# The last projection of a hybrid trunk: seven products over four pairs of output blocks in place of eight, with the outputs kept on chip

## The chip, the cores and the metric

The kernel runs on one core of one Trainium2 chip. A core has five engines that this text calls PE (TensorE, matrix products; its weight loads are shown apart as PEld), DVE (VectorE), ACT (ScalarE), POOL (GpSimd) and SP (SyncE, which here only issues transfers). Each engine works through its own list of instructions in order and waits at semaphores for the others. The metric is the time of one execution in microseconds (us); less is better.

## The reference, cut to what matters

One even layer, one odd layer and a final norm over 1024 positions of width 1024, all in float32. The change concerns the end: the odd layer's output projection with a 2048 x 1024 weight, the residual, and the final norm.

```python
def rmsnorm(x, g):
    xf = x.astype(jnp.float32)
    return xf * lax.rsqrt(jnp.mean(xf * xf, axis=-1, keepdims=True) + RMS_EPS) * g
...
    y = b_gate * conv * jax.nn.silu(g)
    return y @ w_out
...
            h_res = h_res + short_conv_mixer(h, sc_w_in[i], sc_conv_w[i], sc_conv_b[i], sc_w_out[i])
    return rmsnorm(h_res, final_g).astype(out_dtype)
```

## The kernel before

Everything is held transposed: channels on the 128 partitions, positions along the row. Every float32 operand of a product is split into a high part (one ACT copy that rounds) and a low part (one DVE subtraction), and each product of two 128-row blocks is three matmuls: high x high, high x low, low x high. `split_to` does a split (lines 81 and 82, or 84 and 85 with a factor). `tt` on line 229 is every plain two-input operation of DVE and POOL, so the tiles' names tell them apart.

The earlier stages already use seven products in place of eight for a 2 x 2 block product (`run_pairs`, the matmuls of line 686). They leave the odd layer's gated result y as sixteen blocks of 128 x 1024 in DRAM (`y2d`, stored by line 885). The last pair of blocks, 14 and 15, is finished by two DVE multiplications (tiles `K` and `t`) when the last projection has begun.

The last projection is a plain product. The positions are two halves of 512. For each half, and for each of eight output blocks m, two units run, one for each half of the 2048 input rows: a unit loads a weight block of 128 x 1024 from `scout` (line 97, issued by ACT), splits it (`wsplit`: `whi`, `wlo`), and runs 8 x 3 matmuls of 512 columns (`mm_j`, line 933) into one PSUM tile `acc`. `evac_j` then adds the residual block on DVE, squares it on ACT, applies the gain on ACT, and adds the squares up on DVE. The last block of the second half runs in two quarters of 256 columns (`mm_j7`, line 976), so that the norm of one quarter lies beside the products of the other. `rms_work` makes the norm: ones-vector matmuls (line 150), a short chain on DVE and ACT, a broadcasting matmul (line 168) and an ACT copy (line 169). `j_norm` scales and SP stores the result.

The order of everything is the order in which the code is written (`manual_schedule`): each engine's list is filled as the program text runs. In `steps`, while PE runs unit s, the others are given the split of unit s + 1, the load of unit s + 2, and the evacuation of unit s - 1.

Of the kernel before, what the change touches and what calls it, by code (L numbers as in the profile page):

```python
# [8 lines left out]
F32 = mybir.dt.float32  # L9
# [5 lines left out]
P = 128  # L15
T = 1024
# [11 lines left out]
def trunk(ctx: ExitStack, tc: tile.TileContext, a: dict, out: bass.AP):  # L28
# [44 lines left out]
    def act_tiles(k, shape=(T,)):  # L73
        t = act_slot(k, [P, 2, *shape])
        act[k] = (t[:, 0], t[:, 1])
        return act[k]

    def split_to(h, l, src, scale=None, e=None):

        if scale is None:  # L80
            A.activation(h, src, AF.Copy)  # L81
            (e or V).tensor_tensor(out=l, in0=src, in1=h, op=ALU.subtract)  # L82
        else:
            A.activation(h, src, AF.Copy, scale=scale)  # L84
            V.scalar_tensor_tensor(out=l, in0=src, scalar=scale, in1=h, op0=ALU.mult, op1=ALU.subtract)  # L85
# [142 lines left out]
    def tt(e, o, x, y, op):  # L228
        e.tensor_tensor(out=o, in0=x, in1=y, op=op)  # L229
# [689 lines left out]
    def mm_j(m, kk, half):
        def f(u, work):  # L920
            if kk == 0:
                J_["acc"] = acc_tile()
            acc = u.acc = J_["acc"]
            places = spread(work, 3)
            for k in range(8):
                if k in (2, 4, 6):
                    for g in next(places):
                        g()
                n = kk * 8 + k
                h, l = act[n // 2]  # L930
                w1, w2 = u.hi[:, k * P : k * P + P], u.lo[:, k * P : k * P + P]
                for i, (w, x) in enumerate(((w1, h), (w1, l), (w2, h))):
                    PE.matmul(acc[:, 0:512], lhsT=w, rhs=x[:, n % 2], start=n == 0 and i == 0, stop=n == 15 and i == 2)  # L933
        return f

    def fetch_j(m, half):
        def f():
            t = J_["h", m] = slot(f"t{m % 2}", [P, 512])
            LD.dma_start(t, hrd[m][:, 512 * half : 512 * half + 512])
        return f  # L940

    def evac_j(m, half):
        def f(u):
            if m == 0 and half == 0:
                J_["td"] = slot("td0", [P, 4, 512])
            if m % 2 == 0:
                if half and m == 6:
                    J_["o", half, 3] = J_["td"][:, 0:2]
                else:
                    J_["o", half, m // 2] = slot(f"t{2 + 4 * half + m // 2}", [P, 2, 512])  # L950
            o = J_["o", half, m // 2][:, m % 2]
            tt(V, o, u.acc[:, 0:512], J_["h", m], ALU.add)
            q = J_["td"][:, 3 if m == 0 else 2]
            A.activation(q, o, AF.Square)
            A.activation(o, o, AF.Copy, scale=gf[:, m : m + 1])
            if 0 < m:
                tt(V, J_["td"][:, 3], J_["td"][:, 3], q, ALU.add)
        return f
# [5 lines left out]
    def mm_j7(q):
        def f(u, work):
            acc = J_["acc7", q] = acc_tile()[:, 0:256]
            places = spread(work, 15)
            for n in range(16):
                if n:
                    for g in next(places):  # L970
                        g()
                w = units[idx["j", 1, 7, n // 8]]
                k, (h, l) = n % 8, act[n // 2]
                w1, w2 = w.hi[:, k * P : k * P + P], w.lo[:, k * P : k * P + P]
                for i, (wt, x) in enumerate(((w1, h), (w1, l), (w2, h))):
                    PE.matmul(acc, lhsT=wt, rhs=x[:, n % 2, quarter(q)], start=n == 0 and i == 0, stop=n == 15 and i == 2)  # L976
        return f

    def evac_j7(q):
        c = quarter(q)  # L980
        o = J_["o", 1, 3][:, 1, c]
        tt(V, o, J_["acc7", q], J_["h", 7][:, c], ALU.add)
        A.activation(J_["td"][:, 2, c], o, AF.Square)

    def j_rms(c, last):
        def sums():
            if c.start == 0:
                J_["rs"] = slot("rs", [P, 512])
            return [J_["td"][:, 3, c]] + ([J_["td"][:, 2, c]] if last else [])
        return rms_work(sums, lambda: J_["rs"][:, c], c.stop - c.start)  # L990

    def j_norm(half, i, c, e):

        n = c.stop - c.start
        o, r = J_["o", half, i], J_["rs"][:, c]
        if half and i == 3:
            V.scalar_tensor_tensor(out=o[:, 1, c], in0=o[:, 1, c], scalar=gf[:, 7:8], in1=r, op0=ALU.mult, op1=ALU.mult)
            tt(e, o[:, 0, c], o[:, 0, c], r, ALU.mult)
# [39 lines left out]
    for half in range(2):  # L1038
        for m in range(8):
            last = half and m == 7  # L1040
            add(("j", half, m, 0), Unit(scout[m], mm_j7(0) if last else mm_j(m, 0, half), fetch=fetch_j(7, 1) if last else None))
            add(("j", half, m, 1), Unit(scout[8 + m], mm_j7(1) if last else mm_j(m, 1, half),
                                        None if last else evac_j(m, half), fetch=None if last else fetch_j(m, half)))
# [186 lines left out]
    for k in range(4):  # L1230
# [9 lines left out]
    jA, jB, N_ = idx["j", 0, 0, 0], idx["j", 1, 0, 0], len(units)  # L1240
    sc_tail = {1: [lambda: first_of(jA)],
               2: [lambda: [y2_load(0, n, n + 2) for n in range(0, 14, 2)]],
               4: [lambda: [y2_split(0, n) for n in range(4)]],
               5: [lambda: wsplit(units[jA]), lambda: [y2_split(0, n) for n in range(4, 8)]]}
    for i in range(8):
        at(pre, jA + 3 + i, lambda i=i: y2_load(1, 2 * i, 2 * i + 2))
    at(post, jB - 2, lambda: [y2_split(1, n) for n in range(8)])
# [141 lines left out]
    for n in range(8, 12):
        y2_split(0, n)  # L1390

    def first_j():
        late = end2()
        for n in range(12, 14):
            y2_split(0, n)
        for n in range(14, 16):
            late[n - 14]()
            y2_split(0, n, H_["b"][n - 14][:, H0])

    steps(jA, N, first_j)  # L1400
    evac_j7(1)
    for f in rB[1]:
# [71 lines left out]
```

## Time and profile before

| | us |
|---|---|
| median of 3 runs (lowest, highest) | 1636.63 (1634.88, 1636.76) |
| the profiled execution: time | 1635.34 |
| the profiled execution: span from first to last instruction | 1633.5 |
| PE busy in the span | 1581.8 (97%) |
| DVE, ACT, POOL busy in the span | 1074.0, 550.4, 661.3 |
| the last projection and final norm, from its first matmul | 1438.2 to 1633.5 |

The profile is of one execution. Its span leaves out 1.8 us of the time around it. A busy PE is a PE with a matmul in flight; matmuls overlap, so the spacing of their starts tells the pace. A wait is shown in square brackets behind an instruction: how long its engine sat idle before it, and which instruction ended that.

### The profile page before, as it was taken

To read this page: it belongs to the slowest core of one execution; us is meant where nothing else is said; L and a number is where in the kernel's file an instruction comes from. 1 tells how busy PE (TensorE), PEld (TensorE's weight loads), DVE (VectorE), ACT (ScalarE), POOL (GpSimd) and SP (SyncE) were. 2 spreads that over 40 slices of the span, in tenths; PEclk is the share of its full clock that TensorE was granted. 3 is DMA by queue.
4 is the path that set the end of the run, shared out by engine and by line. 5 is a ranking of instruction groups with operands and counts; after the bars stand their busy time and mean duration, and the time that the engine had idled before them with its cause. 6 is when DMAs were issued, how large, how long until landed. Compare 5 with 4: busy or idle time off the path is not lost.

```text
span 1633.5 us, 19047 instructions
## 1 busy us (share of the span) xinstructions
PE 1581.8 (97%) x7186; PEld 1308.3 (80%) x7186; DVE 1074.0 (66%) x1249; ACT 550.4 (34%) x818; POOL 661.3 (40%) x636
## 2 busy tenths in 40 slices
PE   9899999998999999999879999999999999999997
PEld 7688888877888788888658888888888888878886
DVE  6545655688555776661798686968686777763543
ACT  5245211123443433341443232332333332343531
POOL 6852599707422533102455353534343535400001
PEclk9999999999999999999979999999999999999998
DMA  6242632214687432133201212112121212266353
GB/s 213 97 123 91 152 118 84 78 47 148 190 292 228 159 116 78 55 131 132 109 26 52 102 54 78 63 67 77 54 101 52 78 52 78 72 200 205 116 154 117
DMA packets 95035, 181.30 MB, mean 111 GB/s; under 512 B 16352, under 2 KB 52960, under 8 KB 94432
## 3 DMA queue, kind: packets, MB, share of 16 engines
q10 hardware_dynamic: 49664, 116.41, 22.1%
q1 hardware_dynamic: 45280, 63.68, 11.6%
q8 instruction: 57, 0.93, 0.2%
q14 instruction: 34, 0.28, 0.0%
HBM read 141.33 MB, written 42.93 MB: 113 GB/s over the span
## 4 chain that ended last, share of the span: by engine, by line
PE 59%; DVE 5%; issue 1%; DMA 1%; ACT 0%; ACTq 0%; DVEq 0%
PE acc L686 44%; PE acc L933 9%; PE acc L114 4%; PE acc L837 1%; DVE t L229 1%; DVE a L85 1%; DVE ws L82 1%; PE acc L976 1%; DVE a L82 0%; DMA t<-in_glu 0%; DMA hpd<-t 0%; PE aux L168 0%; DVE big L82 0%; ACTq L911 0%; PE aux L150 0%
## 5 line engine op out<-in xcount | busy, mean ns | idle before, releaser
L686 PE MATMUL acc<-a,ws 128*128 128x512 f32 x1920 | 451.3, 391 | 4.0 <-DVE LR L229 1.7
L686 PEld LDWEIGHTS acc<-a,ws 128*128 128x128 f32 x1920 | 361.8, 189 | 81.5 <-ACT a L81 3.1
L114 PE MATMUL acc<-a,whi 128*128 128x512 f32 x1440 | 393.3, 395 | 3.3 <-DVE t L229 2.6
L114 PEld LDWEIGHTS acc<-a,whi 128*128 128x128 f32 x1440 | 268.3, 189 | 58.9 <-issue 4.0
L229 POOL TENSOR_TENSOR t<-t,t 128x512 f32<-128x512 f32 (+2 forms) x81 | 145.6, 1797 | 294.5 <-DVE ws L82 183.7
L686 PE MATMUL acc<-big,ws 128*128 128x512 f32 x960 | 230.9, 396 | 11.6 <-DVE ws L82 4.7
L81 ACT ACTIVATE ws<-t 128x512 fp32r<-128x512 f32 x200 | 125.8, 630 | 338.7 <-PE acc L686 201.5
L82 DVE TENSOR_TENSOR wlo<-raw,whi 128x1024 fp32r<-128x1024 f32 (+2 forms) x89 | 117.2, 1320 | 181.7 <-ACT whi L81 181.7
L686 PEld LDWEIGHTS acc<-big,ws 128*128 128x128 f32 x960 | 182.7, 191 | 53.4 <-DVE ws L82 6.4
L114 PE MATMUL acc<-a,wlo 128*128 128x512 f32 x720 | 222.6, 390 | 0.0
L82 DVE TENSOR_TENSOR ws<-t,ws 128x512 fp32r<-128x512 f32 x200 | 181.5, 908 | 34.0 <-ACT ws L81 32.1
L114 PEld LDWEIGHTS acc<-a,wlo 128*128 128x128 f32 x720 | 136.0, 189 | 28.8
L81 ACT ACTIVATE whi<-raw 128x1024 fp32r<-128x1024 f32 (+2 forms) x89 | 86.7, 977 | 190.1 <-PE acc L114 120.9
L933 PE MATMUL acc<-a,whi 128*128 128x512 f32 x480 | 149.0, 391 | 1.5 <-ACT a L84 1.1
L229 DVE TENSOR_TENSOR t<-t,acc 128x512 f32<-128x512 f32 x134 | 91.1, 681 | 51.0 <-PE acc L686 51.0
L686 PE MATMUL acc<-td,ws 128*128 128x512 f32 x480 | 118.1, 395 | 0.3 <-DVE td L82 0.3
L686 PEld LDWEIGHTS acc<-td,ws 128*128 128x128 f32 x480 | 91.2, 190 | 21.2 <-issue 1.3
L933 PEld LDWEIGHTS acc<-a,whi 128*128 128x128 f32 x480 | 90.0, 188 | 21.6 <-ACT a L84 1.5
L229 POOL TENSOR_TENSOR t<-C,LR 128x1024 f32<-128x1024 f32 (+1 forms) x18 | 42.6, 2372 | 141.3 <-PE aux L491 62.3
L933 PE MATMUL acc<-a,wlo 128*128 128x512 f32 x240 | 93.8, 391 | 0.3 <-DVE wlo L82 0.3
L229 POOL TENSOR_TENSOR t<-t,rs 128x512 f32<-128x512 f32 x5 | 8.7, 1747 | 197.2 <-ACT rs L169 197.2
L229 POOL TENSOR_TENSOR raw<-raw,raw 128x512 f32<-128x512 f32 x20 | 26.7, 1337 | 121.1 <-DVE ws L82 121.0
(260 smaller groups left out, 1945.6 us busy)
## 6 DMA issues: line engine op xcount, KB each, us to landing
raw<-in_scin ACTq DMA_DIRECT2D x32, 512.0 KB, 4.4
t<-in_scin ACTq DMA_DIRECT2D x32, 512.0 KB, 4.2
raw<-in_scout ACTq DMA_DIRECT2D x32, 512.0 KB, 3.7
raw<-in_win ACTq DMA_DIRECT2D x29, 512.0 KB, 3.6
t<-ud ACTq DMA_DIRECT2D x16, 512.0 KB, 4.2
raw<-in_wout ACTq DMA_DIRECT2D x16, 512.0 KB, 3.9
big<-y2d ACTq DMA_DIRECT2D x15, 512.0 KB, 5.8
ud<-t SPq DMA_DIRECT2D x8, 512.0 KB, 3.1
```

The source lines that it names most:

```text
L81: A.activation(h, src, AF.Copy)
L82: (e or V).tensor_tensor(out=l, in0=src, in1=h, op=ALU.subtract)
L85: V.scalar_tensor_tensor(out=l, in0=src, scalar=scale, in1=h, op0=ALU.mult, op1=ALU.subtract)
L114: PE.matmul(acc[:, n * 512 : n * 512 + 512], lhsT=w, rhs=x[:, n * 512 : n * 512 + 512], start=first and i == 0, stop=last and i == 2)
L229: e.tensor_tensor(out=o, in0=x, in1=y, op=op)
L686: PE.matmul(bank, lhsT=wt, rhs=x[:, k], start=k == 0 and j == 0, stop=k == 3 and j == 2)
L837: PE.matmul(u.acc[:, hs], lhsT=w, rhs=x[:, hs], start=k == 0 and j == 0, stop=k == NK - 1 and j == 2)
L933: PE.matmul(acc[:, 0:512], lhsT=w, rhs=x[:, n % 2], start=n == 0 and i == 0, stop=n == 15 and i == 2)
L976: PE.matmul(acc, lhsT=wt, rhs=x[:, n % 2, quarter(q)], start=n == 0 and i == 0, stop=n == 15 and i == 2)
```

## The change

The projection is cut into 2 x 2 blocks. For a pair p of output blocks (2p and 2p + 1) the weight gives A11 (`scout[2p]`), A12 (`scout[8 + 2p]`), A21 (`scout[2p + 1]`) and A22 (`scout[9 + 2p]`); y gives B11 (blocks 0 to 7, first half of the positions), B12 (the same, second half), B21 (blocks 8 to 15, first half) and B22. Seven products of sums of these replace the eight plain ones. The sums of B serve all four pairs, so the order is product by product: product 1 for the four pairs, then 5, 7, 6, 4, 2 and 3 (`JT`). That makes 28 units of 8 x 3 matmuls; product 3 runs in two quarters of 256 columns, its four units twice, which makes 32 steps t = 0 to 31 (`j_slot`).

- `jb_sum`: the sums of B, in place, 8 operations of 128 x 512 for each of products 5, 7, 6 and 4. Half of them stand on POOL, half on DVE; those of product 4 are all on POOL. `jb_split` splits the result, two blocks in a step.
- `jw_sum`: the sums of A, one operation of 128 x 1024 for each of the 16 units of products 5, 7, 6 and 3, all on POOL. Units of products 1, 4 and 2 have none.
- `j_post`: adds a finished product from PSUM to the outputs it belongs to, which stay on chip (`JO`): one ACT copy for product 1; 1, 2, 3, 1, 1 and 1 DVE additions for products 5, 7, 6, 4, 2 and 3.
- `res_add`: the residual, one POOL addition of 128 x 1024 for each output block. `j_sq2`, `j_sq`, `j_norm`: squares, gain and norm as before, in other pieces.
- All loads of the stage are issued by SP instead of ACT, and the output is stored in 24 transfers in place of 12.

```diff
+    JT = (1, 5, 7, 6, 4, 2, 3)
...
+    def jb_sum(i, n, e):
+        if i == 5:
+            tt(e, x0(n), x1(n), x0(n), ALU.subtract)
+        elif i == 7:
+            tt(e, x1(n), b22(n), x1(n), ALU.subtract)
+        elif i == 6:
+            tt(e, x0(n), b22(n), x0(n), ALU.subtract)
+        elif i == 4:
+            tt(e, x0(n), x1(n), x0(n), ALU.subtract)
...
+    def jw_sum(w):
+        i, p = JT[w // 4], w % 4
+        r = J_["raw", w]
+        if i == 5:
+            tt(G, r[0], r[0], r[1], ALU.add)
+        elif i == 7:
+            tt(G, J_["S", p], J_["S", p], r[0], ALU.subtract)
+        elif i in (6, 3):
+            tt(G, J_["S", p], r[0], J_["S", p], ALU.subtract)
...
+        for n in range(8):
+            for f in mid.get(n, []):
+                f()
+            h, l = J_["B", i, n // 2]
+            w1, w2 = wh[:, n * P : n * P + P], wl[:, n * P : n * P + P]
+            for j, (w, x) in enumerate(((w1, h), (w1, l), (w2, h))):
+                PE.matmul(bank, lhsT=w, rhs=x[:, n % 2, c], start=n == 0 and j == 0, stop=n == 7 and j == 2)
...
+        if i == 1:
+            A.activation(q[0], bk, AF.Copy)
+        elif i == 3:
+            tt(V, q[1][:, c], q[1][:, c], bk, ALU.add)
+        else:
+            for d, x in {5: ((1, 0),), 7: ((3, 1), (2, 0)), 6: ((1, 1), (2, 2), (3, 3)), 4: ((2, 2),), 2: ((0, 0),)}[i]:
+                tt(V, q[d], q[x], bk, ALU.add)
...
+    def res_add(m):
+        o = J_["o", m // 2][m % 2]
+        tt(G, o, o, J_["h", m], ALU.add)
...
+    for w in range(4, 28):
+        at(j_pre, w - 2, lambda w=w: jw_sum(w))
+    for w in range(1, 28):
+        at(j_pre, w - 1, lambda w=w: jw_split(w))
+    for w in range(6, 28):
+        at(j_pre, w - 3, lambda w=w: jw_load(w))
+    for x in range(6):
+        i = JT[x + 1]
+        for n in range(8):
+            if x == 0:
+                at(j_pre, n // 2, lambda i=i, n=n: jb_sum(i, n, G if n % 2 else V))
+            at(j_pre, 4 * x + n // 2, lambda i=i, n=n: jb_split(i, n))
+    for x in range(1, 6):
+        for n in range(8):
+            at(j_pre, 4 * x + n // 2 - 1, lambda i=JT[x + 1], n=n: jb_sum(i, n, G if i == 4 or n % 2 else V))
...
+    norm_q(1)
```

POOL's list, of the kernel after, from the first instruction of the last projection: `big` holds B11 and B12, `td` B22, `raw` and the first two `t` of a pair a weight block. Before, POOL had nothing here until the last norm.

```order
L229 TENSOR_TENSOR big_10171<-big_10171 128x512 x2
L229 TENSOR_TENSOR raw_10143<-raw_10143,raw_10145 128x1024
L229 TENSOR_TENSOR big_10171<-big_10171 128x512
L229 TENSOR_TENSOR t_1234_10253<-t_1234_10253,t_1236_10255 128x1024
L229 TENSOR_TENSOR big_10171<-big_10171 128x512
L229 TENSOR_TENSOR big_10171<-td_1246_10339,big_10171 128x512
L229 TENSOR_TENSOR raw_10418<-raw_10418,raw_10420 128x1024
L229 TENSOR_TENSOR big_10171<-td_1246_10339,big_10171 128x512
L229 TENSOR_TENSOR t_1264_10463<-t_1264_10463,t_1266_10465 128x1024
```

The first six rows (seven instructions; the last reads `td`) belong to steps 0 to 3, and six of the instructions need nothing but loaded data: they may run as soon as POOL reaches them. From the row with `td` on, POOL needs the blocks of B22.

DVE's list before, one and a half pairs of units in the middle of the last projection (`wlo` a unit's low part, `t`<-`acc` the evacuation, `td` the sum of squares):

```order
L229 TENSOR_TENSOR t_1240_10366<-acc_10302,t_1236_10333 128x512
L82 TENSOR_TENSOR wlo_10396<-raw_10363,whi_10395 128x1024
L82 TENSOR_TENSOR wlo_10430<-raw_10399,whi_10429 128x1024
L229 TENSOR_TENSOR t_1240_10366<-acc_10370,t_1244_10401 128x512
L229 TENSOR_TENSOR td_1239_10365<-td_1239_10365 128x512
```

DVE's list after, steps 6 to 8 of the 32 (`C`, `B`, `K`<-`acc` is `j_post`, `wlo` the next unit's low part, `a` the low parts of two sums of B, `big`<-`td`,`big` one sum of B):

```order
L229 TENSOR_TENSOR C_1248_10367<-C_1248_10367,acc_10385 128x512
L82 TENSOR_TENSOR wlo_10541<-t_1264_10463,whi_10540 128x1024
L85 SCALAR_TENSOR_TENSOR a_1273_10546<-big_10171,a_1273_10546 128x512 x2
L229 TENSOR_TENSOR big_10171<-td_1252_10382,big_10171 128x512
L229 TENSOR_TENSOR B_1254_10410<-B_1254_10410,acc_10554 128x512
L82 TENSOR_TENSOR wlo_10582<-t_1205_10084,whi_10581 128x1024
L85 SCALAR_TENSOR_TENSOR a_1277_10587<-big_10171,a_1277_10587 128x512 x2
L229 TENSOR_TENSOR big_10171<-td_1246_10339,big_10171 128x512
L229 TENSOR_TENSOR K_10455<-K_10455,acc_10595 128x512
```

What moved: a unit's DVE work grows from one low part and one addition or so to one low part, two low parts of B, a sum of B and an addition from PSUM, and POOL's list beside it is no longer empty.

## Rows read from the trace of the kernel before

**Rows 1.** Last projection: busy us (count) of PE, PEld, DVE, ACT, POOL; clock; DMA; GB/s.

```profile
1452.50:1606.60 154.10, 154.08 (x680) 127.03 (x681) 66.82 (x81) 58.67 (x75) 0.00 (x0) 1.00 0.54 165
```

**Rows 2.** The matmuls with `whi` by line: count, ns min/median/max, first and last start.

```profile
L933 PE MATMUL acc<-a,whi x480: 387/389/799, 1438.2 to 1606.2; 128*128 128x512 f32 x160
...
L976 PE MATMUL acc<-a,whi x64: 277/283/467, 1606.7 to 1619.2; 128*128 128x256 f32 x64
```

**Rows 3.** PE in order of time: 512 columns, then 256 columns (start, duration).

```profile
1589.66 0.62 PE L933 MATMUL acc<-a,whi 128*128 128x512 f32 x2
...
1590.34 0.62 PE L933 MATMUL acc<-a,whi 128*128 128x512 f32 x2
...
1609.17 0.40 PE L976 MATMUL acc<-a,whi 128*128 128x256 f32 x2
...
1609.53 0.40 PE L976 MATMUL acc<-a,whi 128*128 128x256 f32 x2
```

**Rows 4.** The norm's matmuls in the chain that ended last (start, us, what).

```profile
1538.32 0.79 PE aux L150 x8
...
1544.72 0.86 PE aux L168 x2
...
1614.02 0.79 PE aux L150 x8
...
1617.06 0.45 PE aux L168 x2
```

**Rows 5.** The longest wait at the start of the last projection, in order of time.

```profile
1450.31 0.19 PEld L933 LDWEIGHTS acc<-a,whi 128*128 128x128 f32 x1 [1.50 <-ACT a L84]
```

**Rows 6.** DVE's groups by shape from 1460 us on: count, busy us, mean ns.

```profile
L82 DVE TENSOR_TENSOR wlo<-raw,whi 128x1024 fp32r<-128x1024 f32 x28 | 34.3, 1226 | 75.6 <-ACT whi L81 75.6
L85 DVE SCALAR_TENSOR_TENSOR a<-big,a 128x512 fp32r<-128x512 f32 x16 | 9.8, 689 | 0.6 <-ACT a L84 0.6
...
L229 DVE TENSOR_TENSOR t<-acc,t 128x512 f32<-128x512 f32 x13 | 8.9, 684 | 0.0
```

**Rows 7.** Busy time in a stretch in which DVE and POOL both always have work.

```profile
838.00:850.90 12.90, 9.04 (x35) 6.02 (x34) 12.87 (x11) 7.08 (x13) 12.84 (x8) 0.92 0.05 7
```

**Rows 8.** The same stretch in order of time, DVE and then POOL.

```profile
839.92 1.40 DVE L229 TENSOR_TENSOR t<-t,acc 128x512 f32<-128x512 f32 x2
...
842.85 1.78 DVE L82 TENSOR_TENSOR a<-C,a 128x512 fp32r<-128x512 f32 x1
...
841.09 1.29 POOL L229 TENSOR_TENSOR C<-C,LR 128x512 f32<-128x512 f32 x1
842.35 1.73 POOL L229 TENSOR_TENSOR t<-t,C 128x512 f32<-128x512 f32 x1
844.05 1.73 POOL L229 TENSOR_TENSOR K<-K,B 128x512 f32<-128x512 f32 x1
```

**Rows 9.** DVE and POOL with instructions of 1024 columns, in order of time.

```profile
1346.19 0.69 DVE L82 TENSOR_TENSOR ws<-t,ws 128x512 fp32r<-128x512 f32 x1
1347.53 2.69 DVE L874 SCALAR_TENSOR_TENSOR t<-t,t 128x1024 f32<-128x1024 f32 x1 [0.66 <-ACT t L873]
...
1346.35 2.79 POOL L229 TENSOR_TENSOR B<-B,C 128x1024 f32<-128x1024 f32 x1 [4.80 <-DVE C L874]
```

**Rows 10.** DVE when the last projection begins, in order of time.

```profile
1440.50 2.49 DVE L85 SCALAR_TENSOR_TENSOR a<-big,a 128x512 fp32r<-128x512 f32 x4
```

**Rows 11.** The end of the kernel, in order of time.

```profile
1626.53 1.77 POOL L229 TENSOR_TENSOR t<-t,rs 128x512 f32<-128x512 f32 x1 [5.61 <-ACT rs L169]
1628.26 1.17 POOL L229 TENSOR_TENSOR td<-td,rs 128x256 f32<-128x256 f32 x1
1628.77 0.94 DVE L997 SCALAR_TENSOR_TENSOR td<-td,vec,rs 128x256 f32<-128x256 f32 x1
```

**Rows 12.** Transfers by issuer: KB each, median us from issue to landing.

```profile
raw<-in_scout ACTq DMA_DIRECT2D x32, 512.0 KB, 3.7
big<-y2d ACTq DMA_DIRECT2D x15, 512.0 KB, 5.8
```

More of the change, by code (lines that the diff above doesn't have):

```diff
@@ L919, in mm_j @@
[L919 to L958, printed above, removed]
+    J_ = {"T": {}, "o": {}, "w": {}, "raw": {}, "h": {}, "bank": {}, "ring": 0, "acc": [None] * 3}
@@ new lines, in trunk, with jw_load @@
+    JS = ("t9", "t6", "t4", "t5")
+    def jw_load(w):
+        i, p = JT[w // 4], w % 4
+        src = {1: (2 * p,), 5: (2 * p + 1, 9 + 2 * p), 7: (2 * p + 1,), 6: (9 + 2 * p,), 4: (9 + 2 * p,),
+               2: (8 + 2 * p,), 3: (8 + 2 * p,)}[i]
+        r = J_["raw", w] = []
+        for j, m in enumerate(src):
+            ctr[0] += 1
+            if i == 1:
+                t = J_["S", p] = slot(JS[p], [P, T])
+            elif i == 5 and p % 2:
+                t = slot(f"t{j}", [P, T])
+            else:
+                t = wp.tile([P, T], F32, tag="raw", name=f"raw_{ctr[0]}")
+            S.dma_start(t, scout[m])
+            r.append(t)
@@ new lines, in jw_sum, with jw_split @@
+    def jw_sum(w):
+        i, p = JT[w // 4], w % 4
+        r = J_["raw", w]
[5 more added lines that the diff above has]
+            tt(G, J_["S", p], r[0], J_["S", p], ALU.subtract)
+    def jw_split(w):
+        i, p = JT[w // 4], w % 4
+        if i == 3 and p > 1:
+            t = slot(f"td{p - 2}", [P, 2, T], F32R)
+            h, l = t[:, 0], t[:, 1]
+        else:
+            ctr[0] += 1
+            h = wp.tile([P, T], F32R, tag="whi", name=f"whi_{ctr[0]}")
+            l = wp.tile([P, T], F32R, tag="wlo", name=f"wlo_{ctr[0]}")
+        J_["w", w] = (h, l)
+        split_to(h, l, J_["S", p] if i in (1, 7, 6, 3) else J_["raw", w][0])
@@ L961, in quarter, with j_slot @@
+    def j_slot(t):
+        if t < 24:
+            return JT[t // 4], t % 4, slice(0, 512)
+        return 3, t % 4, quarter((t - 24) // 4)
     def quarter(q):
         return slice(256 * q, 256 * q + 256)
[L964 to L977, printed above, removed]
@@ new lines, in j_post @@
+    def j_post(t):
+        i, p, c = j_slot(t)
+        bk = J_["bank", t]
+        if i == 1:
+            J_["o", p] = [slot(g, [P, T]) for g in JO[p]]
+        o = J_["o", p]
+        q = [o[0][:, H0], o[0][:, H1], o[1][:, H0], o[1][:, H1]]
+        if i == 1:
+            A.activation(q[0], bk, AF.Copy)
+        elif i == 3:
+            tt(V, q[1][:, c], q[1][:, c], bk, ALU.add)
+        else:
+            for d, x in {5: ((1, 0),), 7: ((3, 1), (2, 0)), 6: ((1, 1), (2, 2), (3, 3)), 4: ((2, 2),), 2: ((0, 0),)}[i]:
+                tt(V, q[d], q[x], bk, ALU.add)
@@ L985, in j_rms, with j_sq @@
+    def j_sq(p, c, last=False):
+        o, n = J_["o", p][0][:, c], c.stop - c.start
+        sq = slot(("t9" if c.start == 512 else "t6") if last else ("t0", "t2", "t3")[p % 3], [P, 512])[:, :n]
+        A.activation(sq, o, AF.Square)
+        if last:
+            J_["sq"] = sq
+        else:
+            tt(V, J_["ss"][:, c], J_["ss"][:, c], sq, ALU.add)
+        if not last:
+            A.activation(o, o, AF.Copy, scale=gf[:, 2 * p : 2 * p + 1])
     def j_rms(c, last):
         def sums():
-            if c.start == 0:
-                J_["rs"] = slot("rs", [P, 512])
@@ L989, in sums @@
-            return [J_["td"][:, 3, c]] + ([J_["td"][:, 2, c]] if last else [])
+            if "rs" not in J_:
+                J_["rs"] = slot("rs", [P, T])
+            return [J_["ss"][:, c]] + ([J_["sq"]] if last else [])
         return rms_work(sums, lambda: J_["rs"][:, c], c.stop - c.start)
[L992 to L998, printed above, removed]
-        else:
-            tt(e, o[:, :, c], o[:, :, c], r.unsqueeze(1).to_broadcast([P, 2, n]), ALU.mult)
-        t0 = 512 * half + c.start
-        S.dma_start(out[2 * i : 2 * i + 2, :, t0 : t0 + n].rearrange("m p t -> p m t"), o[:, :, c])
@@ L1004, in j_norm_last, with j_norm, at_q @@
-    def j_norm_last(q):
-        for i, e in enumerate((V, V, G, G)):
-            j_norm(1, i, quarter(q), e)
+    def j_norm(m, c, e, last=False):
+        o, r = J_["o", m // 2][m % 2][:, c], J_["rs"][:, c]
+        if last:
+            V.scalar_tensor_tensor(out=o, in0=o, scalar=gf[:, m : m + 1], in1=r, op0=ALU.mult, op1=ALU.mult)
+        else:
+            tt(e, o, o, r, ALU.mult)
+        S.dma_start(out[m, :, c], o)
+    def at_q(q):
+        return slice(512 + 256 * q, 768 + 256 * q)
@@ L1037, in trunk @@
     sc_pairs = [sc_pair(i, j) for i in range(8) for j in range(4)]
[L1038 to L1043, printed above, removed]
     s5["U"] = {}
@@ L1237, in trunk @@
     sc_pe = {1: [rms2[1][0]], 3: [rms2[1][1]]}
[L1240 to L1247, printed above, removed]
@@ new lines, in trunk, with norm_q @@
+    rH, rQ = j_rms(H0, False), [j_rms(at_q(q), True) for q in range(2)]
+    j_mid[26] = {4: [rH[0]]}
+    j_mid[27] = {7: [rH[1]]}
+    for m in range(8):
+        at(j_pre, 28 + m // 2, lambda m=m: j_norm(m, H0, G if m % 2 else V))
+    for q in range(2):
+        for p in range(4):
+            at(j_pre, 25 + 4 * q + p, lambda q=q, p=p: j_sq(p, at_q(q), p == 3))
+    j_mid[29] = {4: [rQ[0][0]]}
+    j_mid[30] = {7: [rQ[0][1]]}
+    def norm_q(q):
+        c = at_q(q)
+        j_norm(6, c, V, True)
+        for m, e in ((7, G), (0, V), (1, V), (2, G), (3, V), (4, V), (5, G)):
+            j_norm(m, c, e)
@@ L1385, in first_fa @@
             next_ya((k,))
-    steps(fa0, jA, first_fa, True)
+    steps(fa0, N, first_fa, True)
     end2 = run_pairs(sc_pairs, "sc", sc_work, sc_pe, sc_tail)
[L1389 to L1402, printed above, removed]
+    late = []
+    for t in range(NS):
+        if t:
+            j_post(t - 1)
+        else:
+            late = end2()
+        for f in j_pre.get(t, []):
+            f()
+        for f in late:
+            f()
+        late = []
+        j_mm(t, j_mid.get(t, {}))
+    j_post(NS - 1)
+    for f in j_pre[NS] + rQ[1]:
         f()
-    j_norm_last(1)
+    norm_q(1)
 def kernel(**inputs):
```

86 lines of the change are left out of this document (64 added, 22 removed).

## The prediction

> **What bounds the kernel now.** I read the windows of the last stage first, because the change touches nothing ahead of it. In [rows 1] the reader is to see that PE is busy for 154.08 of 154.10 us while DVE and ACT work two fifths of the time and POOL not at all: the last projection runs at PE's pace. The pace is in [rows 3]: three matmuls of 512 columns start every 0.68 us (0.2267 each), three of 256 columns every 0.36 us (0.12 each). [Rows 2] count the matmuls of the high weight parts, two of each three: so there are 480 x 3/2 = 720 of 512 columns and 64 x 3/2 = 96 of 256, from 1438.2 us to about 1619.6. Their time is 720 x 0.2267 + 96 x 0.12 = 174.7 us. The norm's own matmuls take 0.79 + 0.86 + 0.79 + 0.45 = 2.9 us of it [rows 4]. The stage lasts 181.4 us on PE, so 3.8 us are waits; they lie at its start, where blocks 14 and 15 of y come late (the longest is 1.50 us [rows 5]). The end behind the last matmul is 13.9 us.
>
> **PE's part of the change.** 24 steps of 24 matmuls of 512 columns are 576 x 0.2267 = 130.6 us (5.44 a step), 8 steps of 24 of 256 columns are 192 x 0.12 = 23.0 us (2.88 a step): 153.6 us, 21.1 less. The waits at the start go too: product 1 needs only blocks 0 to 7, and the late blocks come into use eight steps later. So PE's gain is 21.1 + 3.8 = **24.9 us** if nothing else holds it up.
>
> **What the other engines get.** Counted engine by engine, it fits. In a step of 5.44 us DVE has at most a low part of the weight (1.23), two low parts of B (0.69 each), a sum of B (0.69) and one or two additions from PSUM (0.68 each) [rows 6]: 4.7 us. POOL has a sum of A and one or two half-size sums, 2.4 to 5 us.
>
> But the two do not run side by side. In [rows 7] both are busy for all of 12.9 us, and [rows 8] show how: from 842.35 on POOL's 128 x 512 additions start every 1.70 us, and between two of them exactly one DVE instruction gets done. The DVE row that begins at 842.85 lasts 1.78 us, where it needs about 0.69 alone; it ends 0.55 us after POOL's ends (844.63 against 844.08). POOL's next ends 1.15 us after that. The two DVE instructions at 839.92 that read `acc` in PSUM keep their 0.70 each. So I take it that a DVE instruction with two inputs in SBUF and a POOL instruction exclude each other, and alternate when both are waiting. Of this exclusive time a 512-wide one takes 0.55 us on DVE and 1.15 on POOL. For 1024 columns [rows 9] give it: POOL's instruction ends at 1349.14, 2.26 us after DVE's before it (1346.88), and DVE's next ends at 1350.22, 1.08 later.
>
> [...]
>
> **The sum of the exclusive time.** Now the steps do not fit. In steps 4 to 10 DVE has 1.08 + 3 x 0.55 = 2.73, POOL 2.26 + 1.15 = 3.41: 6.14 us of a 5.44-us step. In steps 11 to 14 (product 4's sums all on POOL) it is 2.18 + 4.56 = 6.74.
>
> It matters when POOL does its part. Its list needs only loaded data at first, later a block of y or a weight (3.7 us to land [rows 12]) or a split of DVE's that is two steps old. So it runs ahead, alternating with DVE one for one: two full-size and two half-size sums fall into one DVE step, which then lasts 6.82 + 2.73 = 9.55 us. I follow it to step 12: by then POOL has done all sums of A through unit 15 (12 x 2.26) and 18 of the 20 half-size sums (18 x 1.15), 47.8 us; DVE has in steps 0 to 11 twelve low weight parts (12 x 1.08), 24 low parts of B and 12 sums of B (36 x 0.55), and the two multiplications for blocks 14 and 15 (2 x 1.08): 34.9 us. Together 82.7 us, against 12 x 5.44 = 65.3.
>
> PE's step 12 needs DVE's low weight part of unit 12, which two low parts (1.1 us) follow in the list, and needs it only for its third matmul (0.45 us later). DVE enters the stage late: at 1440.5 it still splits blocks for the first product [rows 10], 2.3 us after PE's first matmul. To this comes exclusive time in which neither works. Bounds: nothing, if all PSUM additions (6.6 us in these steps) lie under POOL's, as in [rows 8]; 9 us, if none does and POOL's wait for B22 counts too. POOL can't go on into product 7 until blocks 14 and 15 are multiplied, stored and loaded again, about 8 us after the multiplications (loads of `y2d` take 5.8 [rows 12]). I take 5 us, for that wait alone, since [rows 7] show no other loss. PE's delay by step 12: 82.7 - 1.1 + 2.3 + 5 - 0.45 - 65.3 = **23.2 us** (18 to 27). Steps 13 to 18 then run at PE's pace, the POOL work being done, but a delay of PE is not made good.
>
> **The last steps.** In steps 22 to 25 product 3's sums of A and short steps meet: 7.25 + 4.99 + 3.89 + 4.17 = 20.3 us of exclusive time in 2 x 5.44 + 2 x 2.88 = 16.6. DVE's slack of a few us is worth little where steps are short. Bounds 0 and 8 (with the PSUM additions, 2.2, and a wait for the first norm); I take 3.7 + 0.8 = **4.5**.
>
> **The end.** POOL scales three 256-wide blocks, 3 x 1.17 = 3.5 us, in place of 1.77 + 1.17 [rows 11]; begun at 1626.53 they would end at 1630.04, where the last instruction (DVE's, 1628.77 + 0.94) ended at 1629.71. That is 0.3; with twice as many stores to issue behind it I take **+0.6** (0 to 1.2).
>
> Edits at no cost: the loads moved from ACT to SP (ACT has 58.67 busy us in 154.1 [rows 1], SP only issues; a load waits there for a buffer, but the orders that follow belong to later steps), and the bytes loaded, which stay the same but for the residual read once in whole rows.
>
> **Sum.** -24.9 + 23.2 + 4.5 + 0.6 = +3.4 us. The profiled execution took 1635.34 us, 1.3 below the median; on the median the forecast is 1636.63 + 3.4 = **1640.0 us**.
>
> **The rivals.**
> *POOL keeps step with its listing.* If its loads and buffers hold it to the step in which each sum is written, step 12 finds 9.1 us less to wait for (two full-size and four half-size sums fewer, and no other loss): the delay is 82.7 - 9.1 - 1.1 + 2.3 - 0.45 - 65.3 = 9.1, and steps 12 to 14 add 1.3 each: 13. With 3 at the end, the time is 1636.63 - 24.9 + 13 + 3 + 0.6 = **1628.4**. For it: two raw buffers, and loads of B21 queued among the weights on SP. Against: 3.7 us a load is less than a step. This ends on the other side; it decides where the delays stay under 24.3 us together.
> *The exclusion costs nothing:* POOL fits into DVE's waits, and PE is never short: 1636.63 - 24.9 + 0.6 = **1612.3**. For it: engine by engine it fits, and DVE works 43% of the time now. Against: [rows 7, 8].
> *Worse than summed:* all upper bounds, 27 + 8 + 1.2, make **1648**; and PE, waiting a few us at a time, may lose its clock. [...]
>
> **Chances.** Forecast 0.52 (1634 to 1645), POOL in step with its listing 0.23, no cost 0.08, worse 0.17. The range leaves out the case without cost and the upper half of the worst: **1622 to 1651**; the forecast's own is 1634 to 1645. About 0.2%, 3.3 us, is what a measurement of this kernel can tell from no change (its three runs lie 1.9 apart). Faster by more: 0.23 + 0.08 = 0.31. Within: half of the forecast's chance, 0.27. Slower: 0.25 + 0.17 = 0.42.
>
> **What would show it.** In the trace after: 672 matmuls of about the spacing above, with PE waiting for DVE's `wlo` from step 2 on, 18 to 27 us in all before step 12 and hardly any in steps 13 to 18; DVE rows of 1.7 to 3.4 us in place of 0.7 and 1.2 while POOL runs; POOL two or three steps ahead by step 10. The prediction is wrong if DVE's rows keep their length (no exclusion between these shapes), if POOL is seen waiting for weights, or if PE waits for something else: a load, ACT's high part, a bank.

## The result

After the change the kernel takes 1645.91 us (median of four runs, 1643.17 to 1647.71); the kernel before, run beside it, 1636.49 us (1634.88 to 1636.76). The ratio is 1.0058, with an interval of 1.0041 to 1.0076: it became slower by 9.4 us. The profiled execution took 1644.73 us, with a span of 1642.9 where it had 1633.5.

The windows of the last projection come first again (us, then busy us and count of PE, PEld, DVE, ACT and POOL, granted clock, DMA share, GB/s). The first row is the stretch of [rows 1]; the others follow the new stage from its start to its last matmul.

```profile
1452.50:1606.60 154.10, 137.82 (x586) 111.95 (x586) 145.18 (x125) 66.15 (x91) 92.07 (x38) 0.94 0.44 144
1440.00:1508.00 68.00, 59.57 (x241) 46.34 (x239) 63.93 (x49) 21.17 (x31) 43.68 (x21) 0.95 0.53 175
1508.00:1540.00 32.00, 24.60 (x92) 19.32 (x92) 30.86 (x28) 9.44 (x14) 25.87 (x12) 0.89 0.28 92
1540.00:1595.00 55.00, 55.00 (x243) 45.32 (x242) 50.59 (x50) 31.69 (x42) 24.87 (x9) 1.00 0.41 135
1595.00:1628.50 33.50, 29.49 (x216) 28.36 (x215) 28.01 (x42) 14.49 (x26) 16.70 (x10) 0.90 0.25 88
```

PE was busy for 154.08 of these 154.10 us before. Now it waits in the first half and at the end, and only between 1540 and 1595 us is it busy all the time. DVE is busy for 145.18 us where it had 66.82. PE's waits from 1400 us on (what waited, what ended the wait, us in all, times, longest) name what is late:

```profile
PE acc L1018 <- DVE wlo L82: 16.6, 8, 3.8
...
PE acc L1018 <- ACT whi L81: 1.6, 1, 1.6
PE acc L1018 <- DVE a L85: 1.5, 2, 0.9
```

It waits for DVE's low weight parts. DVE's groups by shape from 1440 to 1600 us answer to [rows 6] (count, busy us, mean ns):

```profile
L85 DVE SCALAR_TENSOR_TENSOR a<-big,a 128x512 fp32r<-128x512 f32 x44 | 63.6, 1486 | 2.8 <-ACT a L84 2.8
L82 DVE TENSOR_TENSOR wlo<-t,whi 128x1024 fp32r<-128x1024 f32 x14 | 23.5, 1680 | 3.2 <-ACT whi L81 3.2
...
L229 DVE TENSOR_TENSOR B<-B,acc 128x512 f32<-128x512 f32 x8 | 5.2, 678 | 2.0 <-PE acc L1018 2.0
```

The low parts of B take 1486 ns on the mean where [rows 6] have 689, those of the weight 1680 where they have 1226. The addition that reads `acc` in PSUM keeps its 678. In order of time, in steps 9 to 11, it is the pattern of [rows 8] with 1024-wide instructions in it (start, us; DVE, then POOL):

```profile
1498.85 3.09 DVE L82 TENSOR_TENSOR wlo<-t,whi 128x1024 fp32r<-128x1024 f32 x1
1501.86 4.58 DVE L85 SCALAR_TENSOR_TENSOR a<-big,a 128x512 fp32r<-128x512 f32 x2
1506.36 1.77 DVE L229 TENSOR_TENSOR big<-td,big 128x512 f32<-128x512 f32 x1
1508.06 1.27 DVE L229 TENSOR_TENSOR C<-LR,acc 128x512 f32<-128x512 f32 x2
1509.26 2.18 DVE L82 TENSOR_TENSOR wlo<-t,whi 128x1024 fp32r<-128x1024 f32 x1
...
1500.82 2.27 POOL L229 TENSOR_TENSOR big<-td,big 128x512 f32<-128x512 f32 x1
1503.17 2.72 POOL L229 TENSOR_TENSOR t<-raw,t 128x1024 f32<-128x1024 f32 x1
1505.85 1.74 POOL L229 TENSOR_TENSOR big<-td,big 128x512 f32<-128x512 f32 x1
1507.55 2.81 POOL L229 TENSOR_TENSOR t<-raw,t 128x1024 f32<-128x1024 f32 x1
1510.32 3.95 POOL L229 TENSOR_TENSOR big<-big 128x512 f32<-128x512 f32 x2
```

DVE's two low parts from 1501.86 on last 4.58 us, where two without a POOL sum beside them take 1.28 (1496.44): a half-size (128x512) and a full-size (128x1024) sum of POOL's lie in them. From 1500.82 to 1510.32 POOL always has a next sum. Its sum at 1510.32 belongs to step 11 of the list, while PE, which began step 10 at 1507.16, waits 3.7 us for the low part that DVE ends at 1511.44:

```profile
1511.50 0.50 PE L1018 MATMUL acc<-a,wlo 128*128 128x512 f32 x1 [3.73 <-DVE wlo L82]
...
1528.53 0.50 PE L1018 MATMUL acc<-a,wlo 128*128 128x512 f32 x1 [2.75 <-DVE wlo L82]
```

The second row is step 12's third matmul. Had each step since the first matmul (1439.40) taken 5.44 us, it would have begun at 1439.40 + 12 x 5.44 + 0.45 = 1505.13; it is 23.4 us late. Steps 13 to 24 then start 5.44 us apart, but for one 5.65 us.

At the end, steps 24 and 25 take 4.75 and 7.62 us where 2.88 would do; PE waits 1.64 us for a high part there and 2.26 for a low part. The chain behind it, engine by engine, is product 3's sums of A (POOL), high part (ACT), low part (DVE):

```profile
1587.44 4.55 POOL L229 TENSOR_TENSOR t<-raw,t 128x1024 f32<-128x1024 f32 x1 [7.62 <-DMA raw<-in_scout]
...
1596.24 5.42 POOL L229 TENSOR_TENSOR t<-raw,t 128x1024 f32<-128x1024 f32 x2 [1.88 <-DMA raw<-in_scout]
...
1598.92 1.06 ACT L81 ACTIVATE whi<-t 128x1024 fp32r<-128x1024 f32 x1 [3.52 <-POOL t L229]
...
1600.02 2.72 DVE L82 TENSOR_TENSOR wlo<-t,whi 128x1024 fp32r<-128x1024 f32 x1
```

POOL waits for the weight to land, adds, ACT waits for POOL, DVE for ACT, and DVE's low part takes 2.72 us because POOL's next sum runs beside it.

### The profile page after: what moved, and what is told of

Same layout as the page of the kernel before. It is cut to its first block, busy times and chain, and to the rows that moved or that the text cites. A ratio compares the mean times of both kernels' runs of the same rounds, so it can differ in the third digit from the quotient of the medians.

```text
span 1642.9 us, 19135 instructions
## 1 busy us (share of the span) xinstructions
PE 1573.6 (96%) x7138; PEld 1301.5 (79%) x7138; DVE 1164.3 (71%) x1308; ACT 559.4 (34%) x840; POOL 772.2 (47%) x686
## 4 chain that ended last, share of the span: by engine, by line
PE 54%; DVE 10%; issue 1%; DMA 1%; ACT 1%; POOL 1%; DVEq 0%; ACTq 0%
PE acc L686 44%; PE acc L1018 5%; PE acc L114 4%; DVE a L85 3%; DVE wlo L82 2%; PE acc L837 1%; DVE t L229 1%; DVE big L229 1%; DVE ws L82 1%; DMA t<-in_glu 0%; DVE a L82 0%; POOL t L229 0%; DVE B L229 0%; DMA hpd<-t 0%; PE aux L168 0%
## 5 line engine op out<-in xcount | busy, mean ns | idle before, releaser
L114 PE MATMUL acc<-a,whi 128*128 128x512 f32 x1440 | 395.0, 396 | 2.6 <-DVE t L229 2.6
L229 POOL TENSOR_TENSOR t<-t,t 128x512 f32<-128x512 f32 (+2 forms) x85 | 158.7, 1867 | 302.8 <-DVE ws L82 183.7
L114 PE MATMUL acc<-a,wlo 128*128 128x512 f32 x720 | 222.8, 391 | 0.0
L82 DVE TENSOR_TENSOR wlo<-raw,whi 128x1024 fp32r<-128x1024 f32 (+2 forms) x67 | 92.6, 1386 | 100.1 <-ACT whi L81 100.0
L1018 PE MATMUL acc<-a,whi 128*128 128x512 f32 (+1 forms) x448 | 137.3, 390 | 3.2 <-ACT whi L81 1.6
L229 DVE TENSOR_TENSOR t<-t,acc 128x512 f32<-128x512 f32 x140 | 94.9, 680 | 51.0 <-PE acc L686 50.9
L81 ACT ACTIVATE whi<-raw 128x1024 fp32r<-128x1024 f32 (+2 forms) x67 | 63.5, 952 | 143.7 <-PE acc L114 120.8
L1018 PE MATMUL acc<-a,wlo 128*128 128x512 f32 (+1 forms) x224 | 88.7, 396 | 16.6 <-DVE wlo L82 16.6
L229 POOL TENSOR_TENSOR raw<-raw,raw 128x512 f32<-128x512 f32 (+1 forms) x22 | 32.0, 1455 | 128.3 <-DVE ws L82 121.0
L81 ACT ACTIVATE ws<-raw 128x512 fp32r<-128x512 f32 x80 | 50.0, 626 | 74.4 <-PE acc L686 51.7
```

The source lines that it names most:

```text
L114: PE.matmul(acc[:, n * 512 : n * 512 + 512], lhsT=w, rhs=x[:, n * 512 : n * 512 + 512], start=first and i == 0, stop=last and i == 2)
L1018: PE.matmul(bank, lhsT=w, rhs=x[:, n % 2, c], start=n == 0 and j == 0, stop=n == 7 and j == 2)
```

## The experiments

Theory: a DVE instruction with two inputs in SBUF and a POOL instruction exclude each other (in [rows 8] such a DVE row lasts 1.78 us where 0.69 would do), and POOL, running ahead of its listing, spends DVE's time before step 13. Rivals: DVE simply has too much to do; or what is late is late by its waits for loads, and the stretched DVE rows are a sign of it. Beside the experiments the kernel before took 1637.26 to 1637.71 us, some 1 us more than beside the changed kernel, which was not run again; so a difference from the changed kernel is good to about 1 us.

**All sums on DVE.** POOL keeps the residual's additions and its part of the norm. The edit also lists the sums of A at the end of their step, behind the splits.

```diff
-            tt(G, r[0], r[0], r[1], ALU.add)
+            tt(V, r[0], r[0], r[1], ALU.add)
...
-                at(j_pre, n // 2, lambda i=i, n=n: jb_sum(i, n, G if n % 2 else V))
+                at(j_pre, n // 2, lambda i=i, n=n: jb_sum(i, n, V))
```

> All sums of A and of B are made by DVE, none by POOL; a sum of A stands behind the split and the sums of B in its step. POOL keeps the residual and the norm. Theory (a DVE instruction with two SBUF inputs and a POOL instruction exclude each other): DVE gets 36 more instructions, some 30 us of work, but POOL's 2.26 and 1.15 us go; a step's DVE work is 5.3 to 6.5 us beside PE's 5.44, so PE waits 2 to 6 us in all: 1615 to 1625 us. Rival (DVE simply has too much to do after the change, POOL's work is free beside it): more work on DVE makes it worse, 1655 us or more.

Measured: 1633.52 us (1631.2 to 1635.82), 0.9977 of before (0.9968 to 0.9987): 12.4 us under the changed kernel, so DVE with more work is earlier, against the first rival. But it is some 8 us more than the theory's upper end. Steps 3 to 5 take 7.06, 8.73 and 8.00 us though POOL is idle. DVE's own waits up to 1490 us name the cause of these:

```profile
DVE a L85 <- ACT a L84: 5.6, 8, 0.7
DVE wlo L82 <- ACT whi L81: 4.3, 5, 1.2
```

A sum of B, its high part on ACT and its low part on DVE stand one behind the other in the list, and DVE waits 0.70 us for ACT each of eight times. That chain was not in the estimate; an experiment below takes it away. Steps 8 to 17 lose another 8.5 us together: there DVE is the limit (busy for 31.98 of 32 us from 1520 to 1552), so it does have too much to do in single steps.

**Only the sums of B on DVE.** The edit above without that of `jw_sum`.

> Only the sums of B move from POOL to DVE; the sums of A stay on POOL. Theory of exclusion: 20 x (1.15 - 0.55) = 12 us less exclusive time before step 13, and POOL has less to run ahead with: 1628 to 1636 us. Rival (DVE has too much to do): 12 us more work on DVE, 1650 us or more.

Measured: 1644.09 us (1642.85 to 1644.46), 1.0042 (1.0023 to 1.0061): between the two ranges, so the theory's estimate missed. Only 12 full-size sums are left on POOL before step 14, but they come in bunches: POOL waits 23.2 us for a weight until 1470.86 and 2.9 us until 1476.99, and then has three sums to do. DVE, then POOL, ahead of the low part that step 7 waits for (it lasts 13.43 us):

```profile
1478.15 5.68 DVE L85 SCALAR_TENSOR_TENSOR a<-big,a 128x512 fp32r<-128x512 f32 x2
1483.76 3.43 DVE L229 TENSOR_TENSOR big<-td,big 128x512 f32<-128x512 f32 x2
...
1480.44 5.59 POOL L229 TENSOR_TENSOR t<-t,raw 128x1024 f32<-128x1024 f32 x2
```

Each short DVE instruction waits for a whole full-size sum: two low parts of B cost 5.68 us. So POOL's sum total is not what counted alone: POOL, coming out of these waits for loads with several sums to do, delayed what DVE had next.

**POOL paced.** The same work on the same engines, but POOL begins each step with an addition of one column of that step's low weight part, so that it can't run far ahead.

```diff
+    scr = cp.tile([P, 1], F32, name="scr")
+    for t in range(28):
+        at(j_pre, t, lambda t=t: tt(G, scr, J_["w", t][1][:, 0:1].bitcast(F32), J_["w", t][1][:, 0:1].bitcast(F32), ALU.add))
```

> In each step POOL first makes a 1-column sum that reads the step's low weight part, so that it cannot run further ahead than about half a step; all else as in the changed kernel. If POOL's running ahead costs (my theory): PE's delay before step 13 falls from 25 to 13 us or so, 1631 to 1638 us. If only the total of exclusive time counts, or running ahead helps: 1643 us or more.

Measured: 1633.6 us (1632.04 to 1636.44), 0.9977 (0.9966 to 0.9989), as the theory expected: 12.3 us come back with one instruction more a step. One step, DVE and then POOL:

```profile
1494.07 1.72 DVE L82 TENSOR_TENSOR wlo<-t,whi 128x1024 fp32r<-128x1024 f32 x1
1495.71 1.28 DVE L85 SCALAR_TENSOR_TENSOR a<-big,a 128x512 fp32r<-128x512 f32 x2
1496.92 2.88 DVE L229 TENSOR_TENSOR big<-td,big 128x512 f32<-128x512 f32 x1
...
1495.93 0.51 POOL L229 TENSOR_TENSOR scr<-wlo 128x1 f32<-128x1 f32 x1 [1.23 <-DVE wlo L82]
1496.40 2.85 POOL L229 TENSOR_TENSOR t<-t,raw 128x1024 f32<-128x1024 f32 x1
1499.20 1.75 POOL L229 TENSOR_TENSOR big<-td,big 128x512 f32<-128x512 f32 x1
```

Here DVE's low weight part is held by a half-size sum (1492.96 to 1494.71) and no longer by a full-size one. PE's waits before step 13 are 8.2 us, where the changed kernel has 15.8, and step 13 begins 11.0 us late instead of 25.1. Steps 8 to 10 take 6.23 to 6.34 us, where the sum of exclusive time had 6.14; steps 11 and 12 take 6.35 and 6.32, where it had 6.74.

**No sums of A.** The listing of `jw_sum` is taken out, so this kernel leaves out the sums of A and multiplies plain weight blocks.

> Leaves out the 16 sums of A (the products use the plain weight blocks); DVE's list is unchanged. Theory of exclusion: 12 x 2.26 us less before step 13, the steps fit, PE waits some 4 us at the start and 2 us at the end: 1616 to 1622 us. Rival (DVE has too much to do by itself, in 5.44 us): DVE's list is the same, so the time stays within 3 us of 1646.

Measured: 1618.75 us (1618.24 to 1619.26), 0.9885 (0.9865 to 0.9906), as expected: 27.2 us for 16 sums. It leaves open whether the sums cost by holding up DVE's instructions beside them or by what waits for POOL.

**POOL writes only.** In place of each sum of A, which this kernel leaves out, POOL writes zeros to the same buffer, twice; what waits for POOL stays. Other than the expectation says, POOL's wait for the weight block goes in 12 of the 16 cases: for products 7, 6 and 3 the zeros go to a buffer into which that block is not loaded.

```diff
-            tt(G, r[0], r[0], r[1], ALU.add)
...
+            d = r[0] if i == 5 else J_["S", p]
+            G.memset(d, 0.0)
+            G.memset(d, 0.0)
```

> Each of the 16 sums of A on POOL is replaced by two POOL instructions that only write zeros to the sum's buffer (same place in POOL's list, same waits for loads, same readers behind it, but nothing is read); the sums of A are left out. If DVE is held up by POOL's reading of SBUF while DVE reads two inputs there, the delays of the sums of A are gone as in the run without them: 1617 to 1625 us, DVE's low parts of the weight back near 1.2 us beside a busy POOL. [...]

Measured: 1614.97 us (1614.82 to 1615.13), 0.9864 (0.9845 to 0.9884): below the theory's range, and 20 under the 1635 to 1646 us put at its rival, that whatever POOL does in SBUF holds DVE up, or that the sums cost through the waits that pass through POOL. The time alone doesn't part POOL's reading from its waits for loads; DVE's rows below do. That it is 3.8 us faster than the kernel without sums is a matter of steps 0 to 5: there they lose 7.5 us (step 5 takes 10.07, behind eight half-size sums of B that POOL does in a row from 1456.16 on), here 0.8; a later start of the stage takes part of that back. One step (DVE, then POOL):

```profile
1474.51 1.23 DVE L82 TENSOR_TENSOR wlo<-t,whi 128x1024 fp32r<-128x1024 f32 x1 [0.71 <-ACT whi L81]
1475.65 1.29 DVE L85 SCALAR_TENSOR_TENSOR a<-big,a 128x512 fp32r<-128x512 f32 x2
1476.86 1.78 DVE L229 TENSOR_TENSOR big<-td,big 128x512 f32<-128x512 f32 x1
...
1474.57 0.97 POOL L978 MEMSET t<- 128x1024 f32 x1
1475.60 0.96 POOL L979 MEMSET t<- 128x1024 f32 x1
1476.52 1.56 POOL L229 TENSOR_TENSOR big<-td,big 128x512 f32<-128x512 f32 x1
```

Beside the two writes DVE's rows keep 1.23 and 1.29 (two); beside the sum that reads (1476.52) the next takes 1.78 instead of 0.69.

**Product 3's sums early.** Product 3 uses the weight blocks of product 2; its sums are made from product 2's buffers by DVE.

```diff
-    for w in range(4, 28):
+    for w in range(4, 24):
         at(j_pre, w - 2, lambda w=w: jw_sum(w))
...
+    for w in range(24, 28):
+        at(j_pre, w - 5, lambda w=w: jw_sum(w))
```

> Product 3 uses the same four weight blocks as product 2. Its sums of A are formed from product 2's buffers, on DVE, in steps 19 to 22 in place of 22 to 25, and the four loads of the same blocks go. If the last eight steps lose 7.7 us because product 3's weights come late (loads that wait for a buffer, then POOL, ACT and DVE one behind the other), 5 to 6 us of it come back: 1639 to 1642 us, with less than 3 us lost in the last eight steps. Rival: the short steps are held up by DVE's and ACT's other work for the norms, and the time stays within 1.5 us of 1645.9.

Measured: 1641.42 us (1638.99 to 1642.73), 1.0024 (1.0014 to 1.0033): 4.5 us back. Steps 24 and 25 take 2.87 and 2.95 us, 6.5 less together; steps 22 and 23 take 6.36 and 7.37, 2.9 more, where residual additions on POOL meet the added DVE work. PE waits for no weight from step 24 on. The edit takes away the late loads and POOL's part behind them together; the next run keeps the loads.

**All sums on DVE, a step ahead.** The first experiment, with product 5's sums of B listed a step before their splits. That is the only difference between the two kernels: the sums of A stand behind the splits in both, other than the expectation says.

```diff
+    for n in range(8):
+        at(j_pre, max(0, n // 2 - 1), lambda n=n: jb_sum(5, n, V))
```

> All sums on DVE, as in the first experiment, but the eight sums of B for product 5 stand ahead of the step whose splits use them, and the sums of A ahead of the splits of B. If the first experiment lost its start to the chain sum on DVE, high part on ACT, low part on DVE (0.70 us idle eight times, some 1 us four times more), 5 to 8 us come back: 1626 to 1629 us, with DVE's waits for ACT in the first eight steps under 2 us. Rival: DVE has too much work there in any order, the work of steps 0 to 7 is the limit, and the time stays at 1632 to 1635 us.

Measured: 1624.52 us (1624.12 to 1626.27), 0.9925 (0.991 to 0.9939): 9.0 us under the first experiment, more than expected. Steps 0 to 7 take 43.8 us together, eight times 5.44 being 43.5; in the first experiment they took 51.5. DVE's waits for `a` are gone; those for `whi` (4.5 us, where under 2 were expected) are still there and cost PE nothing. All loads stand where the changed kernel has them, and DVE, which makes the sums now, waits for none of them up to 1600 us, against the second rival. Steps 24 and 25 take 2.87 and 2.88 us.

**All on DVE, spread.** The residual's additions go to DVE too, the sums are spread so that no step is much overfull, with product 3's early as above; the last evacuation goes ahead of four multiplications of the norm.

```diff
+    for i, d in ((5, "00001122"), (7, "44455566"), (6, "778899ab"), (4, "bccdeeff")):
+        for n in range(8):
+            at(j_pre, int(d[n], 16), lambda i=i, n=n: jb_sum(i, n))
...
-        tt(G, o, o, J_["h", m], ALU.add)
+        tt(V, o, o, J_["h", m], ALU.add)
```

> All sums and the additions of the residual on DVE, spread over steps 0 to 23 so that DVE's list takes about 5.3 us of each 5.44 (at most 6.4 in single steps); product 3's sums from product 2's buffers in steps 19 to 22 and two of its splits two steps earlier; the last block's evacuation ahead of four multiplications of the norm before it. If POOL's exclusion and the late weights are all that the change costs, the time is 1612.3 (no cost) plus 1 at the start, 2 to 4 where a step is overfull, about 3 in the short steps, less 1.4 at the end: 1616 to 1622 us. Rival: DVE at 98% of the step is itself late all the time, as in the first experiment: 1628 us or more.

Measured: 1615.97 us (1614.81 to 1616.67), 0.9868 (0.9852 to 0.9884): 30 us under the changed kernel and 1.3% faster than before. The windows of its first 80 us (columns as above):

```profile
1440.00:1460.00 20.00, 20.00 (x90) 16.42 (x89) 20.00 (x27) 8.88 (x14) 0.00 (x0) 1.00 0.72 252
1460.00:1480.00 20.00, 20.00 (x90) 16.57 (x89) 18.15 (x26) 8.98 (x13) 0.00 (x0) 1.00 0.62 208
1480.00:1500.00 20.00, 20.00 (x90) 16.58 (x89) 20.00 (x27) 6.92 (x10) 0.00 (x0) 1.00 0.43 132
1500.00:1520.00 20.00, 20.00 (x89) 16.45 (x89) 19.90 (x28) 6.76 (x10) 0.00 (x0) 1.00 0.43 133
```

DVE is busy for 78 of 80 us and PE for all 80: DVE alone carries it. Its low parts of B take 686 ns on the mean, as in [rows 6].

**Two waits more.** Residual additions moved to steps 16 to 18, product 3's second weight split in step 23.

```diff
-        if i == 3 and p > 1:
+        if i == 3 and p % 2:
...
+        at(j_pre, (16, 17, 17, 18)[p], lambda p=p: res_add(2 * p + 1))
```

> As the run before it (all on DVE, spread), with its two remaining losses taken on: the additions of the residual go from steps 15 to 18, where its trace shows 1.9 us of waits, to steps 16 to 18, and product 3's second weight is split in step 23 into a buffer that is free by then (its trace shows 2.3 us of PE's wait in step 25, where the split had to wait for the buffers of step 23). If these waits are what they seem, 3 to 4 us come back: 1611.5 to 1613.5 us, close to the time without any cost, 1612.3. Rival: DVE, busy for nearly all of the steps, is late elsewhere instead, and the time stays within 1 us of 1616.

Measured: 1615.46 us (1614.26 to 1616.17), 0.9867 (0.9851 to 0.9884): no more than 0.5 us better, inside the spread. The wait of step 25 is gone, but the norm's sum in step 26 now waits instead, as the rival said:

```profile
PE aux L150 <- DVE t L229: 1.3, 1, 1.3
PE aux L150 <- ACT t L1060: 1.0, 1, 1.0
```

## Why the prediction was right, and where it was off

The sign and the mechanism were right: 1640.0 us with 1622 to 1651 was forecast, slower the likeliest side at 0.42, and 1645.91 came. It lies 0.9 us above the forecast's own 1634 to 1645, because part of a rival came true with it: PE's granted clock fell to 0.50 to 0.53 in short stretches. The range's upper end, 1651, lies 3 us above the 1648 of all upper bounds, for a loss of clock; no run shows these 3 us, and in the changed kernel two such stretches cost 1.7 and 2.2 us. Step by step:

- **PE's gain, 24.9 us.** Steps at full pace take 5.44 us, short ones 2.87, as worked out. The trace has 576 + 192 = 768 matmuls, as the working has it; the 672 among its signs was a slip.
- **The exclusion.** Shown: DVE's low parts of B stretch beside POOL's sums (1486 ns on the mean, where [rows 6] have 689), not beside POOL's writes (1.29 us for two), and the additions from PSUM don't stretch (678 ns). The rival without cost (1612.3) is nearly where the kernel arrives when POOL's part of the sums of A doesn't read (1614.97), or when POOL has no sums at all (1615.97).
- **The exclusive time of 1024 columns, 1.08 us on DVE.** As read from [rows 9]: DVE's low weight part that ends at 1511.44 ends 1.08 us behind POOL's sum (1507.55 + 2.81).
- **PE's delay by step 12, 23.2 us.** Measured 23.4 at that matmul. The sum of exclusive time held, but not all the story told with it. POOL was two to three steps ahead of its listing only in step 0, level with it in steps 4 to 6, and one or two ahead from step 7's end on. It waited not 5 but 10.9 us for B22, and 12.7 us for weights, which the prediction had named as a sign of being wrong:

```profile
POOL big L229 <- DMA td<-y2d: 10.9, 1, 10.9
...
POOL raw L229 <- DMA raw<-in_scout: 7.2, 1, 7.2
POOL t L229 <- DMA raw<-in_scout: 4.2, 1, 4.2
POOL t L229 <- DMA t<-in_scout: 1.3, 1, 1.3
```

DVE had work of its own meanwhile. In the 89.0 us up to step 12's low part (1439.4 to 1528.4) only 4.2 us have neither a POOL instruction nor a DVE instruction with two inputs in SBUF, mostly where DVE waits for ACT while POOL waits for a load. DVE's waits in that time are:

```profile
DVE a L85 <- ACT a L84: 2.8, 4, 0.7
DVE wlo L82 <- ACT whi L81: 1.3, 3, 0.7
```

So the 5 us taken for POOL's wait stand for another loss of nearly the same size, the hand-over from DVE to ACT and back. That the total fits so well is partly luck. PE's own waits before step 13 are 15.8 us, where 18 to 27 were expected; what is left of its delay lies mostly behind these waits, where its granted clock is 0.52 to 0.53 (last section).

- **What followed the delay.** Steps 13 to 18 ran at PE's pace, as said. But step 12 itself lost 1.7 us more behind its wait, with a granted clock of 0.53 from 1529.30 to 1532.70, so that step 13 begins 25.1 us late. The forecast's sum had nothing for the clock.
- **The last steps, 4.5 us (0 to 8).** Measured 6.6 us (1.87 in step 24, 4.74 in step 25). Of these 2.2 us are the clock again: from PE's second wait on, the last 22 matmuls of step 25 take 4.86 us, where 2.64 would do.

```profile
1602.79:1607.65 4.86, 4.86 (x22) 4.86 (x23) 4.83 (x4) 1.20 (x2) 2.22 (x1) 0.50 0.02 3
```

The other 4.4 us have the size that was forecast, but the rows of the result show another path than a sum of exclusive time: in short steps a weight that lands late passes through POOL, ACT and DVE one behind the other. With the sums early 0.1 us was left of all 6.6, and with the same loads but the sums on DVE (all sums a step ahead) nothing, so the loads alone are not what makes these steps late.

- **The end, +0.6.** Measured: 14.6 us behind the last matmul (1628.3 to 1642.9) against 13.9, +0.7; but DVE ends last (1638.64), not POOL (1637.69).
- **The start.** Nothing was forecast; the first matmul is at 1439.40, 1.2 us later than before. In the experiments it lies between 1437.58 and 1439.89, also with POOL idle (1439.79 in the first experiment), so it isn't put down to the change.

In sum -24.9 + 1.2 + 25.1 + 6.6 + 0.7 = +8.7 us; the spans differ by 9.4, and so do the medians. Of the 5.9 us by which the forecast was low, the clock behind two waits makes 1.7 + 2.2 = 3.9 and the start 1.2.

The rival that POOL keeps step was put at 1628.4 (its terms add up to 1628.3); the paced kernel comes close to that case, at 1633.6. Its steps 0 to 16 lose 15.5 us in place of 13, with four waits of 0.70 us for ACT in them, which no estimate had, and its last steps lose 5.7, not 3.

## What to carry to other kernels

Moving sums to POOL didn't relieve DVE here, whose instructions beside them read two operands in SBUF (1486 ns where they have 689): add the exclusive time of both engines for each step before counting either as free (by [rows 8] a half-size sum takes 0.55 us of it on DVE and 1.15 on POOL), and let POOL do there what only writes (beside writes DVE's rows kept 1.23 and 1.29 us), or nothing. Where some of it must stay, tie POOL to the pace of the step, since what it did early it took from the step that was due then (the paced kernel's 12.3 us). And where a sum is split right behind it in the list, make the sum a step earlier, so that the hand-over between DVE and ACT, 0.70 us of DVE's waiting each time, lies under other work (9.0 us less, a step ahead).

## What was not expected of the hardware

- POOL's 128x1024 writes of zeros take 0.96 us on the mean, and the DVE rows beside them are not stretched (1.23 us for a low weight part, 1.29 for two of B).
- Behind four of PE's waits (1.92, 3.77, 3.73 and 2.75 us) its granted clock was 0.52 to 0.53 over 3.4 us each and 0.97 to 0.98 in the 3.4 us after, and 0.51 over 6.8 us around two waits close together (1.64 and 2.26). The windows of one such stretch in the changed kernel, behind the 3.73-us wait, and of the paced kernel's steps 0 to 12:

```profile
1512.30:1515.70 3.40, 3.40 (x10) 2.63 (x9) 3.40 (x3) 0.00 (x0) 3.40 (x3) 0.52 0.67 260
```

```profile
1438.00:1520.00 82.00, 73.80 (x316) 58.11 (x315) 79.14 (x69) 29.09 (x42) 62.81 (x39) 1.00 0.50 166
```

In 3.4 us 10 matmuls start, where 15 fit at full pace (0.2267 each). The paced kernel waits 8.2 us of these 82, at most 1.9 us at a time, and keeps 1.00; its longest wait, 2.6 us, lies in step 25, and from 1584 to 1613 it has 0.94. In the changed kernel the three stretches before step 12's wait hardly reached DVE: until then it never waits for PE, and for ACT's `whi`, which PE can hold up, 1.3 us in all. What they cost through later loads isn't shown. The stretch behind that wait costs 1.7 us and the longer one 2.2, since PE waits for nothing there.
